# Two layers and a mixture of experts on one core: tables in steps, splits per residual chunk, both token tiles normalised in turn

## The chip, the core and the metric

The kernel runs on one core of a Trainium2 chip. Five engines work side by side, each through its own queue in order: TensorE (PE: matmuls and transposes into PSUM), VectorE (DVE), ScalarE (ACT), GpSimd (POOL), and SyncE (SP), which issues the transfers. The metric is the device time of one execution in microseconds (us), as the median of several runs; lower is better.

## The reference

256 tokens of width 1024 go through two layers and then a second block, all in float32.

```python
for l in range(DEPTH):                       # first block, DEPTH = 2
    x = x + 0.5 * swiglu_ffn(rms_norm(x, ffn1_norm[l]), ...)   # width 2816
    h = rms_norm(x, mix_norm[l]); proj = h @ w_in[l]
    y_ret = retention(...)                   # 4 heads of 128, rotary, decay
    y_mla = mla_attention(...)               # 8 heads, 64 + 32 rotary, causal
    x = x + jnp.concatenate([y_ret, y_mla], axis=-1) @ w_o[l]
    x = x + 0.5 * swiglu_ffn(rms_norm(x, ffn2_norm[l]), ...)
# second block
attn_o = bidir_gqa(...)                      # 8 query heads, 2 key heads of 64
hgrn_o = hgrn2_bidir(...)                    # gated recurrence, two directions
x = x + (sigmoid(gate_a) * (attn_o @ w_a) + sigmoid(gate_b) * (hgrn_o @ w_b)) @ w_out
x = x + hier_moe(rmsnorm(x, g_ffn), ...)     # 32 experts, top 2
```

## The kernel before

The residual x stays in SBUF as `XT`, features on the partitions (8 chunks of 128), tokens (two tiles of 128) along the free dimension. Weights come in as float32, 1 MB at a time, into four `raw` buffers (`loaded`, L314, issued on SP). `pieces` (L322) splits each into a high part on ACT (`wh`, L332) and a low part, the difference (`wl`, L342), on DVE; in the mixers POOL takes a share of the low part. Four buffers each of `wh` and `wl` lie between the splits and TensorE. Inputs are split the same way: `norm_parts` (L447) multiplies each chunk of `XT` by its gain, ACT writing the high part (L452) and DVE the low part (L453).

The order of the text goes `ffn`, `mixer1`, `ffn` for each layer, then `mixer2` and `moe`. The text alone doesn't fix the queues: a planner runs the instructions through a timeline of its own, and of those that are ready there it takes the one that stands first in the text. Each engine then works through the order so made, strictly in turn.

`ffn` (L493) goes through 11 slices of 256 columns (`f2`), a gate product and an up product in each; `to_residual` (L465) adds the down product to `XT` in four steps of two chunks (L487), squares of the new residual following on POOL (`square`, L408). In the first `ffn` a generator, `load_small` (L160), brings in constants, gains, broadcast rows and router weights, one step per slice from `HOOK_AT` (slice 3) on, each step's transfers placed on SP behind the last weight load issued. Its last step issues three transfers of router weights (L202 to L204) and calls `rotary` (L234), which loads the positions (L235), casts them (L238) and computes sine and cosine tables in some 60 small DVE instructions.

`mixer1` (L552) runs two generators against each other (`interleave`, L304): `mla`, the latent attention, is the main one, and after each of its steps `retention` goes on by about one piece of projection. In `mla` each token tile in turn is normalised (squares on POOL, L641 and L646; sums on DVE, L643 to L647; a reciprocal root by Newton's steps on DVE, `rms_rows`, L399 to L404), rotated (L651 to L660), and transposed on TensorE (`heads_T`, L607). Then come scores, maximum (L688, L689), scaling of the maximum (L690), exponentials, transposes of the probabilities, and their copies out of PSUM (`pt`: L718 on ACT, L719 on DVE). `retention` projects queries and keys, rotates them (`rot`, L740: L745 on POOL, L747 and L748 on DVE, tile `rx`) and transposes them at once.

`mixer2` (L824) does likewise with `attention` (L862), `recurrence` (L1201) and, as filling, `projections`. `mains` takes `NORM_AT` (3) steps of `attention`, then alternates `attention` and `recurrence`; `RATIO_2` (0.4) is the number of projection pieces per step. `recurrence` first pulls the projections that it needs itself. In `attention` each token tile is normalised, rotated, transposed, and copied to `qT` and `kE` (L897 to L904) before the next.

## Time and profile before

| | us |
|---|---|
| median of three runs (1723.22 to 1726.77) | 1724.34 |
| the profiled execution, its own time | 1726.29 |
| its span, first to last instruction | 1724.5 |
| TensorE busy | 1666.9 (97%) |
| DVE busy | 1028.5 (60%) |
| ACT busy | 700.4 (41%) |
| POOL busy | 481.4 (28%) |
| the layers, about | 0 to 1035 |
| mixers of the layers, about | 215 to 332 and 716 to 833 |
| mixer of the second block, about | 1035 to 1250 |
| experts, to the end | from 1250 |

The profile is that of one execution. Busy time is the share of a stretch in which an engine works; the view of waits sums what an engine waited for, by the instruction that released it; the timeline lists instructions in order, with the idle time before each and its releaser in brackets. A wait is put down to the releaser that came last. `PEclk` is the clock granted to TensorE, as a share of its full 2.4 GHz; 0.50 is the lower of its two levels, 1.2 GHz.

### The profile page before, as it was taken

Reading aid. Unit: us, or ns where it says so; the run is one execution under the profiler, and the core shown is the slowest. Engines: PE = TensorE matmul, PEld = TensorE weight load, DVE = VectorE, ACT = ScalarE, POOL = GpSimd, SP = SyncE. Lnnn points to the kernel's source line nnn. Section 1 sums busy time; section 2 is a strip of 40 time slices with the busy share of each in tenths; the row PEclk is TensorE's granted clock in tenths of the full one; section 3 lists DMA queues with packets and bytes.
Section 4 is the critical chain, followed back from the end, with each engine's and each line's share of the span. In section 5 each row is a group of like instructions: output and inputs, shape, how many; then the busy total and the mean of one; then the engine's idle time right before and its main releaser. Section 6 shows DMA issues by size and latency. Waiting matters only on the chain.

```text
span 1724.5 us, 23921 instructions
## 1 busy us (share of the span) xinstructions
PE 1666.9 (97%) x9393; PEld 1258.6 (73%) x9393; DVE 1028.5 (60%) x1631; ACT 700.4 (41%) x1079; POOL 481.4 (28%) x388
## 2 busy tenths in 40 slices
PE   8899988999999999989999999899999999999997
PEld 6788877788888888867888889889844444444442
DVE  6796788876667666787876669975632122122111
ACT  5554465465545554555555445654310000000001
POOL 6333365332222222553422144544400000000000
PEclk9999999999999999999999999999999999999999
DMA  9556542466566555543565555334999999999994
GB/s 313 167 176 198 162 159 83 151 195 190 169 203 182 184 189 173 163 130 100 173 194 190 183 185 166 109 99 147 398 379 400 422 421 422 421 421 422 421 422 178
DMA packets 216600, 407.80 MB, mean 236 GB/s; under 512 B 10063, under 2 KB 177190, under 8 KB 192166
## 3 DMA queue, kind: packets, MB, share of 16 engines
q1 hardware_dynamic: 216486, 406.25, 65.4%
q8 instruction: 75, 1.23, 0.3%
q14 instruction: 39, 0.32, 0.1%
HBM read 405.18 MB, written 1.05 MB: 236 GB/s over the span
## 4 chain that ended last, share of the span: by engine, by line
PE 79%; DVE 14%; issue 3%; POOL 2%; ACT 1%; SPq 1%; DMA 1%; DVEq 0%; POOLq 0%; ACTq 0%
PE mm L360 28%; PE mm L363 14%; PE aux L1507 14%; PE aux L1554 7%; DVE wl L342 4%; PE aux L1490 4%; PE mm L284 2%; PE mm L285 2%; PE mm L286 2%; PE mm L1579 2%; PE aux L123 1%; ACT wh L332 1%; POOL gu L509 0%; DVE XT L487 0%; DVE rx L747 0%
## 5 line engine op out<-in xcount | busy, mean ns | idle before, releaser
L342 DVE TENSOR_TENSOR wl<-raw,wh 128x1024 fp32r<-128x1024 f32 (+5 forms) x392 | 485.3, 1240 | 198.0 <-ACT wh L332 194.4
L332 ACT ACTIVATE wh<-raw 128x1024 fp32r<-128x1024 f32 (+3 forms) x392 | 405.1, 1036 | 356.8 <-PE mm L360 198.6
L360 PE MATMUL mm<-x,wh 128*128 128x512 f32 x1456 | 484.1, 398 | 11.5 <-DVE gu L380 6.5
L363 PE MATMUL mm<-x,wl 128*128 128x256 f32 x1456 | 361.4, 282 | 0.0
L360 PEld LDWEIGHTS mm<-x,wh 128*128 128x128 f32 x1456 | 271.1, 189 | 76.6 <-DVE gu L380 7.6
L363 PEld LDWEIGHTS mm<-x,wl 128*128 128x128 f32 x1456 | 256.0, 189 | 4.2
L360 PE MATMUL mm<-h,wh 128*128 128x512 f32 x704 | 246.6, 393 | 0.0
L1507 PE MATMUL aux<-raw,xg 128*64 128x512 f32 x1024 | 242.1, 598 | 0.0
L509 POOL TENSOR_TENSOR gu<-gu,rb 128x512 f32<-128x512 f32 x88 | 142.0, 1618 | 322.8 <-DVE gu L380 299.7
L363 PE MATMUL mm<-h,wl 128*128 128x256 f32 x704 | 196.4, 279 | 0.0
L1507 PEld LDWEIGHTS aux<-raw,xg 128*64 128x64 f32 x1024 | 76.2, 137 | 137.1 <-issue 131.9
L360 PEld LDWEIGHTS mm<-h,wh 128*128 128x128 f32 x704 | 131.9, 187 | 31.3
L342 POOL TENSOR_TENSOR wl<-raw,wh 128x352 fp32r<-128x352 f32 (+2 forms) x90 | 119.5, 1334 | 84.3 <-ACT wh L332 76.1
L363 PEld LDWEIGHTS mm<-h,wl 128*128 128x128 f32 x704 | 131.9, 187 | 0.0
L1554 PE MATMUL aux<-raw,hd 128*64 128x512 f32 x512 | 124.8, 594 | 0.0
L383 ACT ACTIVATE yp<-aux 128x512 fp32r<-128x512 f32 x32 | 19.1, 597 | 245.8 <-PE aux L1554 231.2
L1492 DVE TENSOR_TENSOR xg<-aux,gperm 128x256 f32<-128x256 f32 x64 | 27.0, 423 | 142.6 <-PE aux L1490 142.6
L1554 PEld LDWEIGHTS aux<-raw,hd 128*64 128x64 f32 x512 | 42.2, 137 | 69.1 <-issue 66.5
L1490 PEld LDWEIGHTS aux<-gg,hk 128*128 128x128 f32 x512 | 61.6, 196 | 31.0 <-issue 29.8
L285 PE MATMUL mm<-wl,x 128*128 128x512 f32 (+2 forms) x208 | 79.6, 386 | 2.6 <-DVE wl L342 2.5
L384 DVE TENSOR_TENSOR yp<-aux,yp 128x512 fp32r<-128x512 f32 x32 | 22.1, 691 | 97.2 <-ACT yp L383 97.2
L284 PE MATMUL mm<-x,wh 128*128 128x256 f32 x272 | 79.3, 292 | 0.0
(400 smaller groups left out, 2364.3 us busy)
## 6 DMA issues: line engine op xcount, KB each, us to landing
raw<-in_w_exp_gate_dram SPq DMA_DIRECT2D x64, 1024.0 KB
raw<-in_w_exp_up_dram SPq DMA_DIRECT2D x64, 1024.0 KB
raw<-in_w_exp_down_dram SPq DMA_DIRECT2D x62, 1024.0 KB
raw<-in_ffn_w_up_dram SPq DMA_DIRECT2D x44, 1024.0 KB
raw<-in_ffn_w_gate_dram SPq DMA_DIRECT2D x43, 1024.0 KB
raw<-in_w_in_dram SPq DMA_DIRECT2D x36, 1024.0 KB
raw<-in_ffn_w_down_dram SPq DMA_DIRECT2D x32, 1024.0 KB
raw<-in_ffn_w_down_dram SPq DMA_DIRECT2D x16, 768.0 KB
```

Of the source, the lines that this page charges most:

```text
L284: nc.tensor.matmul(ps, a[0], b[0], start=first, stop=False, skip_group_check=True)
L285: nc.tensor.matmul(ps, a[0], b[1], start=False, stop=False, skip_group_check=True)
L286: nc.tensor.matmul(ps, a[1], b[0], start=False, stop=last, skip_group_check=True)
L332: nc.scalar.activation(h, r[:, k0:k1], AF.Copy)
L342: eng.tensor_tensor(lf, rf, hf.bitcast(F32), op=ALU.subtract)
L360: nc.tensor.matmul(banks[j], lhs, chunk_both(xp, kk), start=kk == 0, stop=False, skip_group_check=True)
L363: nc.tensor.matmul(banks[j][:, :S], lhs, chunk(xp, kk)[0], start=False, stop=kk == k_all - 1, skip_group_check=True)
L509: nc.gpsimd.tensor_tensor(e, e, twice(rb), op=ALU.mult)
L1490: nc.tensor.matmul(ps[:, i], hk[:, t, (k0 + i) * P:(k0 + i + 1) * P], gs[t], start=i == 0 and t == 0, stop=i == 1 and t == 1, skip_group_c ...
L1507: nc.tensor.matmul(ps[half(s)], xg[:, k, half(s)], w[s][:, k % 4], start=k == 0, stop=k == 7, skip_group_check=True)
L1554: nc.tensor.matmul(pss[hf][half(s)], hd[:, ff, half(s)], w[s][:, ff - ks.start, hf * 512 - c0:(hf + 1) * 512 - c0], start=ff == 0, stop=ff ...
L1579: nc.tensor.matmul(osum[t][hf], gt[:, t * P:(t + 1) * P], yp[part][:, hf], start=False, stop=p == NP - 1 and part == 1, skip_group_check=True)
```

## The change

- `load_small` starts at slice 2 (`HOOK_AT`), yields between the router's transfers and the tables, and `rotary` is a generator itself: one step for the positions and first reductions, one for the second, one for each of cosine and sine, one for the copies.
- `norm_parts` is divided: `into_parts` splits one chunk. `to_residual` gets the next stage's gain and calls it for the two chunks that it has just finished, before their squares. `norm_parts` does what is left.
- In `mla` the norms of both tiles come first, then both rotations (with `kf`), then the transposes of both. The factor of the scores goes into the gain of the queries; the maximum comes out negated; `ptb` is copied by ACT.
- In `retention` the transposes of `rx` are put off (`turns`) and run after the first piece of the next projection.
- In `attention` of the second block both tiles are normalised, then both rotated, then both transposed. The factor goes into the copy to `qT`; the copies to `kx` and `kE` go from DVE to ACT; the maximum comes out negated. `NORM_AT` is 6, and the steps under it run at `RATIO_N` = 1.5 pieces each.
- In the recurrence a factor goes from two products into `homs`, so that two `scalar_tensor_tensor` in each direction become `tensor_tensor`.

```diff
+RATIO_N = 1.5
-HOOK_AT = 3
-NORM_AT = 3
+HOOK_AT = 2
+NORM_AT = 6
...
         late.update(cst=cst, gcol=gcol, rw=rw, gperm=gperm)
+        yield
 
         nc.gpsimd.tensor_tensor(rw, rw, gains("g_ffn_2", 0)[:, :, None].to_broadcast([P, 8, 40]), op=ALU.mult)
-        rotary()
+        yield from rotary()
...
             nc.vector.scalar_tensor_tensor(n1, nh, -4096.0, n1, op0=ALU.mult, op1=ALU.add)
+            yield
             for c in parts:
...
             for i, (shift, add) in enumerate(((0.25, math.pi / 2), (0.0, 0.0))):
+                yield
                 whole(n1, ang, 1 / (2 * math.pi), shift)
...
+    parts_of, ahead = {}, []
+
+    def into_parts(g, k):
+
+        if k == 0:
+            parts_of["x"] = [pair_tile(np_, [P, 4, S], "x%d" % i, bufs=1) for i in range(2)]
+        xh, xl = chunk(parts_of["x"], k)
+        x = x_banks[k // 2][:, k % 2] if x_banks else XT[:, k]
+        nc.scalar.activation(xh, x, AF.Copy, scale=g[:, k:k + 1])
+        nc.vector.scalar_tensor_tensor(xl, x, g[:, k:k + 1], xh.bitcast(F32), op0=ALU.mult, op1=ALU.subtract)
+
...
+            if g is not None:
+                for k in (2 * d2, 2 * d2 + 1):
+                    into_parts(g, k)
+                    ahead.append(k)
             if final:
                 square(2 * d2)
...
                     rms_rows(ms, 32.0, 24)
-                    yield
+                    mss.append(ms)
+                    yield
+                for t in range(2):
+                    q, kv, ms = qs[t], vv[t], mss[t]
...
-                    yield
                     nc.vector.tensor_tensor(kf[t][:, :, 0:64], kv[:, :, 0:64], ms[:, 8:16, None].to_broadcast([P, 8, 64]),
                                             op=ALU.mult)
-                    heads_T(qT, q, t, "qn_nope")
+                    yield
+                for t in range(2):
+                    heads_T(qT, qs[t], t, "qn_nope")
                     yield
                     heads_T(kT, kf[t], t, "kn_nope")
                     yield
...
-                    nc.vector.tensor_reduce(mx[:, 0:2], s0, axis=AX.X, op=ALU.max)
-                    nc.vector.tensor_reduce(mx[:, 2:4], s1, axis=AX.X, op=ALU.max)
-                    nc.vector.tensor_scalar(mx[:, 0:4], mx[:, 0:4], -scale, None, op0=ALU.mult)
+                    nc.vector.tensor_reduce(mx[:, 0:2], s0, axis=AX.X, op=ALU.max, negate=True)
+                    nc.vector.tensor_reduce(mx[:, 2:4], s1, axis=AX.X, op=ALU.max, negate=True)
...
-                    nc.vector.tensor_copy(ptb, tb)
+                    nc.scalar.activation(ptb, tb, AF.Copy)
...
-                    ps2 = aux_bank().rearrange("p (h t) -> p h t", h=4)
-                    for h in range(4):
-                        flip(ps2[:, h], x[:, h], ident)
-                    nc.scalar.activation(dst[:, :, t * P:(t + 1) * P], ps2, AF.Copy)
+
+                    def turn():
+                        ps2 = aux_bank().rearrange("p (h t) -> p h t", h=4)
+                        for h in range(4):
+                            flip(ps2[:, h], x[:, h], ident)
+                        nc.scalar.activation(dst[:, :, t * P:(t + 1) * P], ps2, AF.Copy)
+                    turns.append(turn)
...
+            def then_turns(gen):
+
+                for i, _ in enumerate(gen):
+                    while i == 0 and turns:
+                        turns.pop(0)()
+                    yield
...
-                    nc.vector.tensor_copy(kx, x[:, 8:10][:, ::-1])
+                    nc.scalar.activation(kx, x[:, 8:10][:, ::-1], AF.Copy)
...
-                    nc.vector.tensor_copy(kE[0:64, :, 0, ts], ps[0:64, 0:2])
-                    nc.vector.tensor_copy(kE[64:128, :, 1, ts], ps[64:128, 0:2][:, ::-1])
-                    yield
+                    nc.scalar.activation(kE[0:64, :, 0, ts], ps[0:64, 0:2], AF.Copy)
+                    nc.scalar.activation(kE[64:128, :, 1, ts], ps[64:128, 0:2][:, ::-1], AF.Copy)
+                    yield
...
-                nc.vector.scalar_tensor_tensor(flat(qp), flat(hq), scale, flat(qp), op0=ALU.mult, op1=ALU.mult)
+                nc.vector.tensor_tensor(qp, hq, qp, op=ALU.mult)
...
                 rec = recurrence()
+                rate[0] = RATIO_N
                 for _ in range(NORM_AT):
                     next(att)
                     yield
+                rate[0] = RATIO_2
```

## Rows read from the trace of the kernel before

**Rows 1.** The page's totals: busy us, share of the span, instructions, by engine.

```profile
PE 1666.9 (97%) x9393; PEld 1258.6 (73%) x9393; DVE 1028.5 (60%) x1631; ACT 700.4 (41%) x1079; POOL 481.4 (28%) x388
```

**Rows 2.** Stretches: start:end, length, busy per engine, granted clock, DMA share, GB/s.

```profile
80.00:82.00 2.00, 1.52 (x4) 1.23 (x5) 1.97 (x5) 0.00 (x0) 1.17 (x1) 0.50 0.70 170
...
240.00:260.00 20.00, 17.09 (x74) 13.28 (x75) 19.83 (x38) 8.22 (x9) 13.43 (x11) 0.99 0.41 132
258.00:262.00 4.00, 2.53 (x10) 2.32 (x11) 3.96 (x5) 1.25 (x2) 3.99 (x4) 0.69 0.00 0
272.00:284.00 12.00, 12.00 (x83) 10.57 (x82) 5.05 (x11) 5.22 (x8) 2.97 (x3) 1.00 0.16 49
400.00:420.00 20.00, 20.00 (x115) 17.41 (x114) 13.42 (x17) 11.54 (x18) 5.17 (x4) 1.00 0.64 203
768.00:772.00 4.00, 4.00 (x22) 3.76 (x21) 3.72 (x14) 2.75 (x5) 0.44 (x1) 0.57 0.43 133
1092.00:1096.00 4.00, 4.00 (x20) 3.91 (x19) 3.93 (x6) 3.97 (x6) 3.09 (x2) 0.53 0.58 170
...
1128.00:1132.00 4.00, 4.00 (x22) 3.19 (x21) 2.58 (x4) 2.28 (x6) 2.36 (x2) 0.50 0.06 9
1400.00:1420.00 20.00, 20.00 (x98) 9.32 (x99) 3.87 (x10) 1.10 (x3) 0.00 (x0) 1.00 1.02 424
```

**Rows 3.** Timeline, 64 to 84 us: start, us, engine, line, [idle before, releaser]; SP, DVE, PE.

```profile
64.57 5.16 SPq L202 DMA_DIRECT2D gperm<-in_g_ffn_dram  x1
...
73.72 2.13 SPq L235 DMA_DIRECT2D posi<-in_positions_dram  x1
...
77.59 0.19 DVE L238 CAST pos<-posi 128x2 f32<-128x2 int32 x1 [6.65 <-DMA posi<-in_positions_dram]
...
80.48 3.78 PE L360 MATMUL mm<-x,wh 128*128 128x512 f32 x8 [4.88 <-DVE gu L380]
```

**Rows 4.** TensorE's waits, 205 to 345 us: total, times, longest.

```profile
PE aux L123 <- DVE q L660: 2.9, 2, 2.7
...
PE aux L123 <- DVE rx L748: 1.4, 2, 0.7
PE mm L728 <- DVE pt L719: 1.3, 1, 1.3
```

**Rows 5.** The same for 700 to 845 us.

```profile
PE aux L123 <- DVE rx L748: 5.1, 3, 3.4
...
PE mm L728 <- DVE pt L719: 1.1, 1, 1.1
```

**Rows 6.** The same for 1020 to 1245 us.

```profile
PE aux L913 <- DVE kE L903: 5.0, 1, 5.0
PE aux L123 <- DVE mx L917: 3.3, 1, 3.3
...
PE aux L123 <- DVE kx L899: 1.3, 1, 1.3
```

**Rows 7.** DVE by line and shape, whole span: count, busy us, mean ns, idle before.

```profile
L719 DVE COPY pt<-aux 128x256 f32<-128x256 f32 x8 | 3.3, 413 | 0.0
...
L690 DVE TENSOR_SCALAR mx<-mx 128x4 f32<-128x4 f32 x8 | 2.5, 313 | 0.1
...
L903 DVE COPY kE<-aux 64x256 f32<-64x256 f32 x2 | 0.8, 408 | 0.0
```

**Rows 8.** Timeline, 255 to 263 us, POOL and DVE.

```profile
255.66 3.38 POOL L745 TENSOR_TENSOR rt<-rx,sinr 128x512 f32<-128x512 f32 x2
...
257.85 1.23 DVE L404 SCALAR_TENSOR_TENSOR nwy<-nwt,nwy 128x24 f32<-128x24 f32 x1
...
262.45 0.17 DVE L404 SCALAR_TENSOR_TENSOR nwy<-nwt,nwy 128x24 f32<-128x24 f32 x1
```

**Rows 9.** Timeline, 326 to 335 us, DVE and PE.

```profile
326.28 1.37 DVE L453 SCALAR_TENSOR_TENSOR x<-XT,gcol,x 128x256 fp32r<-128x256 f32 x2
...
334.21 0.50 PE L360 MATMUL mm<-x,wh 128*128 128x512 f32 x1 [1.07 <-DVE x L453]
```

More of the change, by code (lines that the diff above doesn't have):

```diff
@@ L445, in row_broadcast @@
         return rb
-    def norm_parts(g):
-        xp = [pair_tile(np_, [P, 4, S], "x%d" % i, bufs=1) for i in range(2)]
-        for k in range(8):
-            xh, xl = chunk(xp, k)
-            x = x_banks[k // 2][:, k % 2] if x_banks else XT[:, k]
-            nc.scalar.activation(xh, x, AF.Copy, scale=g[:, k:k + 1])
-            nc.vector.scalar_tensor_tensor(xl, x, g[:, k:k + 1], xh.bitcast(F32), op0=ALU.mult, op1=ALU.subtract)
+    parts_of, ahead = {}, []
[6 more added lines that the diff above has]
+        nc.vector.scalar_tensor_tensor(xl, x, g[:, k:k + 1], xh.bitcast(F32), op0=ALU.mult, op1=ALU.subtract)
+    def norm_parts(g):
+        for k in range(len(ahead), 8):
+            into_parts(g, k)
+        ahead.clear()
         for k2, b in enumerate(x_banks):
@@ L463, in wview, with to_residual @@
         return w.rearrange("(k p) n -> p k n", p=P)
-    def to_residual(wsrc, kc, yp, scale, final=True, between=None):
+    def to_residual(wsrc, kc, yp, scale, final=True, between=None, g=None):
         src = wview(wsrc)
@@ L521, in ffn @@
                         next(hook, None)
-            run(to_residual(wd, 22, hp, 0.5))
+            run(to_residual(wd, 22, hp, 0.5, g=g_next()))
     def proj_tok(wsrc, c0, n, xp, use):
@@ L566, in mixer1 @@
                 gtab[nm] = (tcos, tsin)
+            gcols = {"qn_nope": m.tile([P, 1], F32, name="gqs", bufs=1), "kn_nope": gains("kn_nope", l, 1)}
+            nc.gpsimd.tensor_scalar(gcols["qn_nope"], gains("qn_nope", l, 1), 96.0 ** -0.5, None, op0=ALU.mult)
             cmask = m.tile([P, P], BF16, name="cmask", bufs=1)
@@ L612, in heads_T @@
                     nc.scalar.activation(dst[:96, h0:h0 + 4, t * P:(t + 1) * P], ps[:96], AF.Copy,
-                                         scale=gains(gname, l, 1)[:96])
+                                         scale=gcols[gname][:96])
             def mla():
@@ L667, in mla @@
                     yield
-                scale = 96.0 ** -0.5
                 po = None
@@ L766, in retention @@
                 yield
-                yield from proj_tok(w_in, 512, 512, xp, rot(rkT))
+                yield from then_turns(proj_tok(w_in, 512, 512, xp, rot(rkT)))
                 yield
-                yield from proj_tok(w_in, 1024, 512, xp, use_v)
+                yield from then_turns(proj_tok(w_in, 1024, 512, xp, use_v))
                 yield
@@ L820, in mixer1 @@
             share[0] = 0.0
-            run(to_residual(w_o[512:], 4, yp[1:], 1.0))
+            run(to_residual(w_o[512:], 4, yp[1:], 1.0, g=gains("ffn2_norm", 8 * l)))
     def mixer2():
@@ L874, in attention, with room @@
                 nc.gpsimd.memset(kE, 0.0)
+                mss = []
+                def room():
+                    return m.tile([P, 16, 64], F32, tag="A1", name="xr", bufs=1)[:, :10]
                 for t in range(2):
-                    ts = slice(t * P, (t + 1) * P)
-                    x = xa[t]
-                    xr = m.tile([P, 16, 64], F32, tag="A1", name="xr", bufs=1)[:, :10]
+                    x, xr = xa[t], room()
                     nc.gpsimd.tensor_tensor(xr, x[:, 0:10], x[:, 0:10], op=ALU.mult)
@@ L882, in attention @@
                     rms_rows(ms[:, :10], 64.0, 10)
-                    nc.vector.tensor_tensor(x[:, 0:10], x[:, 0:10], ms[:, :10, None].to_broadcast([P, 10, 64]),
+                    mss.append(ms)
+                    yield
+                for t in range(2):
+                    x, xr = xa[t], room()
+                    nc.vector.tensor_tensor(x[:, 0:10], x[:, 0:10], mss[t][:, :10, None].to_broadcast([P, 10, 64]),
                                             op=ALU.mult)
-                    yield
                     for nm, hs, n in (("q_norm_2", slice(0, 8), 8), ("k_norm_2", slice(8, 10), 2)):
@@ L893, in attention @@
                     yield
+                for t in range(2):
+                    x, ts = xa[t], slice(t * P, (t + 1) * P)
                     ps = aux_bank().rearrange("p (a t) -> p a t", a=4)
@@ L970, in mixer2 @@
             nc.vector.tensor_tensor(hup, hom, lb, op=ALU.add)
+            homs = m.tile([P, 2, 4], F32, name="homs", bufs=1)
+            nc.vector.tensor_scalar(homs, hom, scale, None, op0=ALU.mult)
             def times_sigmoid(z, i):
@@ L1086, in direction @@
                 nc.scalar.activation(qi, b, AF.Exp)
[L1087 removed]
+                nc.vector.tensor_tensor(qi, hq, qi, op=ALU.mult)
                 dd = m.tile([P, 4, 4], F32, name="dd")
```

27 lines of the change are left out of this document (14 added, 13 removed).

## Prediction

> **What bounds the kernel now.** I read four views in this order. The totals of the page come first: TensorE is busy for 1666.9 of 1724.5 us, DVE for 60% of the span [rows 1]. A span that is 97% matmul can't be shortened by saving work on other engines in general; it can lose only the 57.6 us in which TensorE has nothing to do, and the time in which it works at its lower clock. So the second view is the table by stretches [rows 2]: the last part of the span (row 1400:1420) has TensorE busy without a gap and the DMA share at 1.02. That part, the experts, is fed by weight transfers without pause, and the change doesn't touch it. Its first loads wait for the memory of the stage ahead of it, so what is saved ahead of it should reach the end of the span one for one. The feed-forward stretches have no idle TensorE at all (row 400:420, with 20.00 of 20; the 18 rows of that view from 340 to 700 us are alike in this). What remains is the start, the two mixers of the layers and the mixer of the second block. There the row 240:260 shows DVE at 19.83 of 20 us while TensorE is idle for 2.9: DVE sets the pace in those stretches, not in the mean of 60%. The third view is the list of waits of TensorE in the three mixers [rows 4 to 6]; the fourth is the timeline around the longest of them.
>
> **The start: tables in steps.** DVE runs its queue in order. The first instruction of the rotary tables, the cast L238, waited 6.65 us for the transfer of the positions, which stood at the end of a row of small transfers on SP: the first was issued at 64.57 and took 5.16 us to issue, the positions were issued from 73.72 to 75.85 [rows 3]. Splits of weights stood behind that cast, and TensorE stood still for 4.88 us; after that it ran at a granted clock of 0.50, the lower of its two levels (row 80:82 of [rows 2]), where the next 3.78 us did the work of 1.9. So the event costs 4.9 + 1.9 = 6.8 us. The change puts a step between these transfers and the positions, so that the slow issues go behind the weights of one slice and the positions behind those of the next. HOOK_AT goes from 3 to 2, so the transfers ahead of it (constants, gains, rows) each come one slice earlier. With the 11.3 us of issue (64.57 to 75.85) shortened to the 2.13 us of the positions alone, the cast should find its data or wait about 1 us. The tables' instructions stay the same in number and are spread over five slices; what stands behind them on DVE is the next split, which now meets one fifth of them at a time. Each SP transfer that is moved forward goes behind a weight load, and four raw buffers keep the loads up to two slices ahead of their use, so I cost the move at 0; if that cover is gone, I bound it by the 4.9 us that the old order lost. POOL's multiplication of the router's weights moves a step behind its transfers and so waits for less. I take 6 of the 6.8 us.
>
> **Input splits per residual chunk.** This moves 8 ACT and 8 DVE instructions per normalisation from the text behind the residual to the text within it, five times. The rows say that the planner had already done so: the L453 of the next stage ran at 326.28, 5 us ahead of the end of the residual, and only one wait of 1.07 us is left behind it [rows 9]. I cost this at 0, with bounds of -1 and +1 us at each of the two places where a mixer ends (elsewhere there is no wait to gain). The squares run on POOL and keep their place there; the sum that waits for them is needed two products later.
>
> **The mixers of the layers.** Two things change: the transposes of the rotated queries and keys (rx) go a step behind, after the first piece of the next projection, and both token tiles are normalised before either is transposed. The waits that answer to it are 2.9 (q L660), 1.4 (rx) and 1.3 (pt) in the first layer [rows 4], 5.1 (rx) and 1.1 (pt) in the second [rows 5]. The granted clock adds to this. In 258:262 it was 0.69: a share of (1 - 0.69)/0.5 = 0.62 of 4 us at half speed, half of which is lost, 1.2 us; in 768:772 it was 0.57, by the same way 1.7 us [rows 2]. That makes 5.6 + 1.2 = 6.8 and 6.2 + 1.7 = 7.9 us. The pt waits should go: the copy L719 leaves DVE for ACT (8 x 0.413 us), and the scaling L690 is gone (8 x 0.313) [rows 7]. The other waits are only half real. DVE was full in that stretch, so moving a transpose back lets TensorE go on only as long as split weights lie ready; beyond that it waits for splits instead. What speaks for a gain is the slack behind the stretch: in 272:284 DVE was busy for 5.05 of 12 us [rows 2], and in the new order 32 transposes that need no DVE fall there. I take half: 3.4 and 4.0 us, with bounds from -6 (below) to the full 14.7.
>
> Here one rule speaks against the change. A reciprocal-root step of 0.17 us took 1.23 us while POOL's rt L745 ran from 255.66 to 259.04 [rows 8]. The Trainium skill (SBUF — State Buffer, Who interferes with whom) says that an instruction of DVE with two inputs in SBUF waits out a POOL instruction that reads SBUF, whole, and the other way round. The trace agrees for that one. By that rule, taking both tiles' squares on POOL next to each other, with two chains of small steps on DVE, would lengthen these chains rather than hide them; by it alone the mixers would give nothing or lose. That is the second rival.
>
> **The mixer of the second block.** TensorE waited 5.0 us for kE L903, 3.3 at mx L917 and 1.3 for kx [rows 6]; the clock of 0.53 in 1092:1096 and of 0.50 in 1128:1132 [rows 2] adds 1.9 and 2.0. Together 13.5 us. The change takes kE and kx off DVE (ACT writes them; two copies L903 of 0.41 us [rows 7], and two L904 of the same shape) and drops the eight scalings L917 (half of L690's shape, so under 0.3 us each). It normalises both tiles in the first six steps, against 1.5 pieces of projection each (before: three steps at 0.4, the rest among the recurrence). The number of pieces ahead of the recurrence is the same, since it pulls the projections that it needs itself; but the second tile's norm leaves the crowded stretch. The four scale-and-multiply instructions become plain products of the same size: 0. I expect the kE wait to go nearly whole (5.0 + 1.9, take 5), kx 1, and of the later stall, which is a full DVE and not one copy, 1. Sum 7 us, bounds 0 and 13.5. ACT, which takes over the copies, was itself full in 1092:1096 (3.97 of 4) [rows 2]; hence 5 of the 6.9.
>
> **The sum.** 6 + 0 + 3.4 + 4.0 + 7 = 20.4 us. The profiled execution took 1726.29 us, 1.8 more than its span; that gives 1705.9. The median of the three runs lies 2.0 below that execution, so the forecast is **1704 us**.
>
> **The rivals.**
> First, *the waits move*: DVE stays the bound in all mixers, and TensorE waits for splits where it waited for transposes. Then only the start (6) and about half of the work that DVE loses count: 3.3 (L719) + 2.5 (L690) + 1.6 (L903, L904) = 7.4, half 3.7. Time 1724.3 - 9.7, about 1715. For it: DVE at 19.83 of 20. Against it: the slack right behind.
> Second, *slower*: the two chains of norms in turn keep DVE from splitting. A chain has 13 small steps; at 1.23 instead of 0.17 us each it is 13.8 us longer, which is the bound; at half of that 6.9, with the lower clock's 1.7, 8.6 us per layer. Two layers: 17.2, against the 13 us of start and second block: 1724.3 - 13 + 17.2 = 1728.5. It decides from 6.5 us per layer on. Against it: the chain of the second tile already ran beside the first's in the trace, since the L404 at 257.85 [rows 8] is one of its steps and stands between the first tile's rope instructions.
> Third, *the change does not do what it says*: each queue's order is made by a planner from its own timeline, and the text only sets priorities. If the cast keeps its place behind an earlier gap and the mixers their order, only the 3.7 us of DVE work are saved: 1721.
> Fourth, *all of it*: every wait named goes, with its clock: 6.8 + 6.8 + 7.9 + 13.5 = 35.0, time 1689.
>
> **How the numbers follow.** Forecast (1697 to 1711) 0.47; waits move (1711 to 1718) 0.20; all of it (1687 to 1697) 0.14; doesn't do it (1717 to 1722) 0.09; slower (1726 to 1740) 0.10. The range 1690 to 1722 leaves out the slower case and some of the best one. A change of 0.2% (3.4 us) is about what a measurement of this kernel can tell from none. Faster by more than that: 0.85 (the forecast, the waits moved and all of it make 0.81, and about half of the case at 1721); within it 0.06; slower 0.09.
>
> **What would show it.** Right: no wait of DVE for the positions beyond 2 us and no granted clock under 1 near 80 us; rx, q and kE gone from TensorE's waits; the experts' stage as long as before and begun about 20 us earlier. Wrong: waits of TensorE for wl L342 in the mixers in place of the others; small steps of DVE (L402 to L404) with a longer mean; the lower clock at new places; loads of the first feed-forward that land late because constants went ahead of them.

## The result, and the profile after

The changed kernel took **1737.14 us** (median of six, 1732.01 to 1737.74), the kernel before in the same session 1724.3 (six, 1723.22 to 1726.77). The ratio is 1.0068, with a 95% interval from 1.0058 to 1.0079: **slower** by 0.7%, where 1704 was forecast and 1722 was the upper end. The profiled execution took 1736.47 us, its span is 1734.7. Below, each ratio is against the kernel before as run on the same chip beside the experiment; its profile is always the one of 1724.5 us.

DVE and POOL did get less work, as [rows 1] against the totals after show: DVE 1028.5 to 1019.8 us, POOL 481.4 to 476.6. ACT, which took over copies, went from 700.4 to 705.5.

```profile
PE 1672.2 (96%) x9393; PEld 1264.9 (73%) x9393; DVE 1019.8 (59%) x1602; ACT 705.5 (41%) x1093; POOL 476.6 (27%) x390
```

TensorE's 9393 instructions are as many as before, but it was busy 5.3 us longer, and the clock below shows why. To see where, I took the end of each stage's last product and read one row per stage (these ends are exact; the table of times had put the mixers at about 215 and 1035). The columns are those of [rows 2]. The rows are, in order: first feed-forward from 20 us on, mixer of layer 0, mixer of layer 1, mixer of the second block up to the router. The kernel before:

```profile
20.00:206.66 186.66, 180.07 (x1018) 156.81 (x1017) 137.90 (x206) 92.11 (x140) 65.86 (x45) 0.98 0.62 195
206.66:331.85 125.19, 115.45 (x616) 93.90 (x614) 105.09 (x182) 69.71 (x131) 66.69 (x60) 0.99 0.40 129
707.17:831.62 124.45, 115.45 (x616) 94.61 (x614) 102.94 (x182) 69.89 (x131) 69.61 (x60) 0.99 0.41 130
1020.07:1251.85 231.78, 219.14 (x1636) 205.56 (x1634) 181.35 (x298) 112.49 (x161) 113.05 (x90) 0.97 0.53 186
```

The changed kernel:

```profile
20.00:209.34 189.34, 180.49 (x1018) 156.69 (x1017) 138.02 (x206) 92.31 (x139) 65.45 (x45) 0.98 0.61 193
209.34:337.18 127.84, 116.92 (x615) 96.46 (x614) 102.39 (x174) 71.00 (x135) 67.80 (x61) 0.96 0.39 126
712.37:837.32 124.95, 116.11 (x615) 95.56 (x614) 100.64 (x174) 71.51 (x135) 69.36 (x61) 0.97 0.41 129
1025.65:1262.99 237.34, 222.39 (x1635) 207.91 (x1634) 177.79 (x285) 114.42 (x167) 107.95 (x90) 0.96 0.54 191
```

The differences of the lengths are +2.7 (start), +2.7, +0.5 and +5.6 us; the other feed-forwards together and the experts gave back 0.2 and 1.0. That is the 10.2 us by which the spans differ. Length less busy is idle time: it grew by 2.3, 1.2 and 2.3 us in the first, second and fourth stage and was the same in the third (9.0 and 8.8). The rest, 0.4, 1.5, 0.7 and 3.3 us, is busy time. Summed over rows of 2 us as busy time times (1 - granted clock), what the lower level took went from 1.4 to 4.7 us in the first mixer, from 1.5 to 3.1 in the second and from 5.6 to 8.8 in the third. That is an estimate, and in the layers' mixers more than the busy time grew by; it shows that the clock is enough to explain it. Each kernel has one profile here, and two profiles of the same queues differ by up to 1.5 us in such a stage (last section), so the stages only point at the places; the experiments decide.

**The start.** The cast still waits. Timeline of the changed kernel (SP, DVE, PE), to be held against [rows 3]:

```profile
53.96 4.70 SPq L203 DMA_DIRECT2D gperm<-in_g_ffn_dram  x1
...
62.38 2.00 SPq L324 DMA_DIRECT2D raw<-in_ffn_w_gate_dram  x1
64.48 0.53 SPq L324 DMA_DIRECT2D raw<-in_ffn_w_up_dram  x1
65.06 1.42 SPq L237 DMA_DIRECT2D posi<-in_positions_dram  x1
...
73.93 0.17 DVE L240 CAST pos<-posi 128x2 f32<-128x2 int32 x1 [4.55 <-DMA posi<-in_positions_dram]
...
75.08 2.08 PE L365 MATMUL mm<-x,wh 128*128 128x512 f32 x4 [4.99 <-DVE gu L385]
...
119.41 2.22 PE L365 MATMUL mm<-x,wh 128*128 128x512 f32 x8 [1.08 <-DVE gu L385]
```

The stretch in which the positions were under way, and TensorE's waits from 40 to 130 us (total, times, longest):

```profile
66.00:74.00 8.00, 4.09 (x26) 3.51 (x24) 1.90 (x3) 2.12 (x4) 1.51 (x2) 0.91 1.09 350
...
PE mm L365 <- DVE gu L385: 7.3, 5, 5.0
```

The positions were issued 8.7 us earlier than before, and behind two weight loads of 1 MB each, issued at 62.38 and 64.48. Their issue ended at 66.48; the cast ran 7.4 us later, at 73.9. Before, their issue ended at 75.85, the last weight load ahead of them had been issued at 64.14, and the cast ran at 77.59. Issued 8.7 us earlier, they let the cast run only 3.7 us earlier. DVE came to it 1.6 us earlier and waited 4.55 us instead of 6.65, and TensorE stood still as long as before, 4.99 us against 4.88. The Trainium skill (DMA: Bandwidth & Descriptors, Queues, rings and completion order) says that each of the 16 engines takes the descriptors of SP's transfers in ring order. By that rule a small transfer has its turn behind the megabytes ahead of it. The trace agrees in the main: in 66 to 74 us the transfers moved 350 GB/s, at which 2 MB take 6.0 of the 7.4 us (an estimate).

That explains why nothing was gained. The loss is in what follows: where one wait of 4.9 us was all before, four more of 0.21 to 1.08 us come behind it, up to the one at 119.41, 7.3 us in all. They make the 2.3 us of idle time by which this stage grew.

**The mixers.** TensorE's waits in the changed kernel (total, times, longest), from 205 to 345 us, against [rows 4]:

```profile
PE aux L124 <- DVE rx L770: 6.0, 3, 4.6
PE aux L124 <- DVE y L841: 3.1, 2, 1.9
```

and from 1020 to 1270 us, against [rows 6]:

```profile
PE aux L124 <- DVE pb L964: 10.4, 3, 4.8
...
PE aux L955 <- ACT kE L946: 0.2, 1, 0.2
```

Of the waits that the prediction named, those for q (2.9), kE (5.0, now 0.2), kx and mx are gone. The one for pt is gone in the first layer (1.3); in the second it went from 1.1 to 0.9 us, now for ACT's copy. The wait for rx, named too, is not gone: it grew from 1.4 to 6.0 us in the first layer and stayed at 5.1 in the second. New are waits for y, the output of the retention, in the layers, and for pb, the probabilities, in the second block.

### The profile page after: what moved, and what is told of

The parts are those of the page before. It is cut to its first block, busy times and chain, and to the rows that moved or that the text cites. A ratio compares the mean times of both kernels' runs of the same rounds, so it can differ in the third digit from the quotient of the medians.

```text
span 1734.7 us, 23889 instructions
## 1 busy us (share of the span) xinstructions
PE 1672.2 (96%) x9393; PEld 1264.9 (73%) x9393; DVE 1019.8 (59%) x1602; ACT 705.5 (41%) x1093; POOL 476.6 (27%) x390
## 4 chain that ended last, share of the span: by engine, by line
PE 82%; DVE 11%; issue 2%; POOL 2%; ACT 2%; DMA 1%; SPq 0%; DVEq 0%; POOLq 0%; ACTq 0%
PE mm L365 28%; PE mm L368 14%; PE aux L1553 14%; PE aux L1600 7%; PE aux L1536 4%; DVE wl L347 4%; PE mm L291 3%; PE mm L289 3%; PE mm L290 3%; PE mm L1625 2%; PE aux L124 2%; ACT wh L337 1%; POOL gu L526 1%; DMA posi<-in_positions_dram 1%; PE aux L708 0%
## 5 line engine op out<-in xcount | busy, mean ns | idle before, releaser
L347 DVE TENSOR_TENSOR wl<-raw,wh 128x1024 fp32r<-128x1024 f32 (+5 forms) x392 | 490.8, 1254 | 209.3 <-ACT wh L337 204.8
L291 PE MATMUL mm<-wh,x 128*128 128x512 f32 (+2 forms) x208 | 79.7, 385 | 0.0
L289 PE MATMUL mm<-wh,x 128*128 128x512 f32 (+2 forms) x208 | 79.2, 392 | 0.3 <-ACT wh L337 0.3
```

The costliest lines, as they stand in the source:

```text
L289: nc.tensor.matmul(ps, a[0], b[0], start=first, stop=False, skip_group_check=True)
L291: nc.tensor.matmul(ps, a[1], b[0], start=False, stop=last, skip_group_check=True)
L347: eng.tensor_tensor(lf, rf, hf.bitcast(F32), op=ALU.subtract)
```

## The experiments

All are the kernel before with one part of the change, unless they say otherwise.

**Three parts, each alone.** First the start:

```diff
-HOOK_AT = 3
+HOOK_AT = 2
...
+        yield
 
         nc.gpsimd.tensor_tensor(rw, rw, gains("g_ffn_2", 0)[:, :, None].to_broadcast([P, 8, 40]), op=ALU.mult)
-        rotary()
+        yield from rotary()
```

> The kernel before with only the start of the change: load_small in more steps, the rotary tables as a generator, HOOK_AT 2. Theory: the start's loss is of this part alone. The positions now go behind the weights of one more slice and wait for their transfers (after: issued 65.06 to 66.48, landed at 73.93, a wait of 4.55 us on DVE), and the tables' steps then meet a DVE without slack until 116 us. So the first feed-forward ends about 2.7 us later (209.3 instead of 206.7), nothing changes later, time +2.7 us, about 1727. Rival: the loss at the start comes from the splits per residual chunk, and the steps by themselves gain what was forecast: first feed-forward ends at about 201, time about 1718.

Measured: 1727.81 us, ratio 1.0018 (1.0008 to 1.0028); the first feed-forward ended at 208.47, and TensorE's waits up to 130 us were 6.3 us in four pieces. The loss at the start belongs to this part.

Then all edits to the layers' mixers:

```diff
+                for t in range(2):
+                    q, kv, ms = qs[t], vv[t], mss[t]
...
-                    nc.vector.tensor_scalar(mx[:, 0:4], mx[:, 0:4], -scale, None, op0=ALU.mult)
...
-                    nc.vector.tensor_copy(ptb, tb)
+                    nc.scalar.activation(ptb, tb, AF.Copy)
...
+                    turns.append(turn)
```

> The kernel before with all edits to the mixer of the layers (both tiles normalised, then rotated, then transposed; transposes of rx a step behind; ptb copied by ACT; the scaling of the maximum folded away), and nothing else. Theory: this part alone makes what the two mixers lost in the changed kernel: first mixer 127.8 us from the end of its feed-forward instead of 125.2, second 125.0 instead of 124.5; time +3 us, about 1727. Rival: the mixer's loss in the changed kernel came from another part (input splits per chunk, or the later start); then these edits give 0 to -7 us, time 1717 to 1724.

Measured: 1728.27 us, ratio 1.0019 (1.0009 to 1.0029). Waits in the first mixer as in the changed kernel: rx 6.0, y 3.1; its length was 127.57 us, that of the second 124.24. But the profiled execution was the fastest of the ten, 1722.89 us, so the profile doesn't show what the median lost.

And all edits to the second block's mixer:

```diff
+RATIO_N = 1.5
...
-NORM_AT = 3
+NORM_AT = 6
...
+                    mss.append(ms)
+                    yield
...
+                    nc.scalar.activation(kE[0:64, :, 0, ts], ps[0:64, 0:2], AF.Copy)
```

> The kernel before with all edits to the mixer of the second block (both tiles normalised in the first six steps, at 1.5 pieces each; kE and kx copied by ACT; factors folded), and nothing else. Theory: this part makes the 5.3 us that the stage lost: from 231.5 to about 237 us between the end of the last feed-forward and the router, since the softmax of the attention now runs at the same time as the recurrence's large instructions (TensorE waited 10.4 us for pb); time +5, about 1729. Rival: the loss came from the input splits per residual chunk or from what stood before; then the stage takes 224 to 231 us and the time is 1717 to 1724.

Measured: 1731.24 us, ratio 1.0042 (1.0025 to 1.0059), with waits for pb of 10.5 us in a stage of 234.89. The excesses of the three parts add up to 0.79%, the whole change has 0.68%: within the intervals the loss is theirs.

**The residual chunks.**

```diff
+            if g is not None:
+                for k in (2 * d2, 2 * d2 + 1):
+                    into_parts(g, k)
+                    ahead.append(k)
```

> The kernel before; the only edit is the input splits per finished residual chunk. Theory: nothing changes, since the planner had put these splits there already: ratio 0.9993 to 1.0007, the same wait of 1.1 us for x behind each layer's mixer. Rival: it costs 1 to 2 us where the other parts' sum (1.0018, 1.0019 and 1.0042) is over the whole (1.0068), that is, the parts don't add: ratio under 0.999.

Measured: 1.0000 (0.999 to 1.0009). That term of the sum, 0, holds, and for the reason given: in the trace every engine has the same instructions in the same order as in the kernel before.

**The start: positions or steps.** The transfer alone is moved:

```diff
             cst.append((lo, hi, t))
+        nc.sync.dma_start(posi, A["positions"].rearrange("o (t p) -> p (o t)", p=P))
         yield
...
     def rotary():
-        nc.sync.dma_start(posi, A["positions"].rearrange("o (t p) -> p (o t)", p=P))
```

> The kernel before; the only edit is that the transfer of the positions is issued in the first step of load_small, with the constants, instead of in the last. Theory: the cast of the positions then finds its data, TensorE's wait of 4.88 us and the stretch at half clock behind it (1.9 us) go, the first feed-forward ends near 200 instead of 206.7 and the time is 5 to 7 us less, about 1718. Rival: DVE has no slack between 84 and 120 us, so the tables' 60 instructions are late next: TensorE idles there in pieces, and the first feed-forward ends at 204 to 207, time 1722 to 1724.

Measured: 1722.03 us, ratio 0.998 (0.9969 to 0.9992); the first feed-forward ended at 203.48. Its timeline (DVE, PE):

```profile
64.50 0.16 DVE L238 CAST pos<-posi 128x2 f32<-128x2 int32 x1
...
83.94 1.19 PE L360 MATMUL mm<-x,wh 128*128 128x512 f32 x4 [1.45 <-DVE gu L380]
```

The cast waits for nothing and no lower clock shows in this stage. But TensorE now waits in four pieces (0.75, 1.45, 0.47 and 0.50, together 3.2 us between 71 and 114) where it waited once for 4.9. The theory was right about the wait and the clock, the rival about the pieces and the time: the event is worth 3.2 us in the end of the stage. That the rest of its 6.8 is the tables' own work fits the rows, in which DVE is busy for 28.9 of the 30 us from 80 to 110, but no run isolates it.

Then the same with the steps of the change (the two diffs above together, except that the positions' line goes):

> The start of the change (more steps, HOOK_AT 2) and the positions issued with the constants. Theory: the steps lost only because the positions' transfer stood behind two megabytes of weights; with the positions early the cast finds its data and the start is no worse than with the positions early and the old steps (0.998): ratio 0.996 to 0.998, first feed-forward ends at 201 to 203.5. The tables' instructions stand one or two between two splits with the old steps already, so the steps by themselves change nothing there. Rival: the steps by themselves lose (transfers moved ahead of weights, waits of 2.3 us in pieces from 94 to 120 us): ratio 0.999 to 1.001, first feed-forward ends at 204 to 206.

Measured: 0.9981 (0.9971 to 0.9991), end of the first feed-forward 204.20: the same ratio as without the steps. The ratio is just above the theory's range, the end lies in the rival's. The steps by themselves show no worth. The traces show why: from the cast on, two to six instructions of the tables stand between two splits with the steps, and two to six did before.

**The layers' mixers, edit by edit.** The turns:

```diff
-                yield from proj_tok(w_in, 512, 512, xp, rot(rkT))
+                yield from then_turns(proj_tok(w_in, 512, 512, xp, rot(rkT)))
```

> The kernel before; the only edit is that the transposes of rx in the retention of the layers go a step behind (turns). The layer mixers' edits together gave 1.0019. Theory: this edit loses: a transpose that stands behind the next piece of projection still waits for an rx that DVE finishes late (6.0 us of waits for rx in the first mixer with all edits, 1.4 before), and the piece in between takes splits from the same DVE. Waits for rx 4 to 6 us per mixer in place of rx and q, ratio 1.001 to 1.002 (2 to 3 us slower). Rival: the loss is of the order of the norms in mla, and the turns by themselves take away 1 to 3 us of waits: ratio 0.998 to 0.9995.

Measured: 1.0000 (0.9991 to 1.001). Neither theory nor rival: rx keeps 1.4 us in the first mixer and has 4.6 in the second (5.1 before), q grows from 2.9 to 4.4, and the stages stay as long (125.20 and 124.75).

The order of the norms:

```diff
-                    yield
+                    mss.append(ms)
+                    yield
+                for t in range(2):
+                    q, kv, ms = qs[t], vv[t], mss[t]
```

> The kernel before; the only edit is the order in mla of the layers: both tiles normalised, then both rotated, then transposed. Theory: the loss is of the turns, so this edit by itself is within 0.1% of the kernel before; the q wait of 2.7 us becomes smaller and another wait takes its place. Rival: the two chains of norms in turn hold up DVE's splits and rotations; TensorE idles 11 us and more in the first mixer instead of 9.3 to 9.9, ratio 1.001 to 1.002.

Measured: 1729.23 us, ratio 1.0027 (1.0016 to 1.0037); the first mixer took 129.58 us, with 10.4 idle. The six microseconds of rx come from this edit (waits, then three stretches of that kernel):

```profile
PE aux L123 <- DVE rx L753: 6.0, 3, 4.7
PE aux L123 <- DVE y L812: 1.2, 1, 1.2
```

```profile
296.00:300.00 4.00, 2.67 (x18) 1.51 (x16) 2.79 (x8) 4.00 (x13) 1.71 (x3) 1.00 0.81 253
300.00:304.00 4.00, 2.79 (x17) 2.36 (x18) 3.26 (x5) 1.65 (x3) 0.69 (x1) 0.75 0.41 139
304.00:308.00 4.00, 4.00 (x16) 3.11 (x14) 1.76 (x4) 0.60 (x2) 0.00 (x0) 0.50 0.00 0
```

The prediction's own picture of this loss, longer small steps, isn't what is seen: those on 128x24 (L399 to L404 of the kernel before) took 16.1 us in all here, 16.7 before and 17.0 in the changed kernel. One wait of 4.7 us for rx replaces those for q and for the step behind it, and a second spell of low clock follows 40 us later. Of the 4.4 us by which the stage is longer, idle time has 0.7; the rest is busy time, at the lower clock. Why the order costs that second spell was not isolated.

Copies and folded factors of all three mixers, without a change of order or pace (the layers' two are shown below):

```diff
-                    nc.vector.tensor_copy(kx, x[:, 8:10][:, ::-1])
+                    nc.scalar.activation(kx, x[:, 8:10][:, ::-1], AF.Copy)
```

> The kernel before with only the copies that move from DVE to ACT (ptb, kx, kE) and the factors folded away (scaling of the maxima, gain of the queries, qT, homs) in all three mixers; no order or pace is changed. Theory: less work on DVE shortens the mixers a little, since DVE is full there: 7.4 us of DVE work less, of which about a third shows: ratio 0.997 to 0.999 (2 to 5 us), waits for pt and kE gone. Rival: the planner reorders around it and the gain is lost in new waits: ratio 0.9995 to 1.002.

Measured: 1728.74 us, ratio 1.0023 (1.0013 to 1.0032): the rival, a little above its range. The second block's mixer became shorter, 227.8 us, and the layers' mixers longer, 131.3 and 127.4. So the layers' part was divided once more. The copy:

```diff
-                    nc.vector.tensor_copy(ptb, tb)
+                    nc.scalar.activation(ptb, tb, AF.Copy)
```

> The kernel before; the only edit is that the second half of the transposed probabilities (ptb, L719) is copied out of PSUM by ACT instead of DVE. Theory: this copy is what made the layers' mixers slower in the run with copies and folds (there 131.3 and 127.4 us for the two mixers, 125 to 127.5 and 124.5 before): ACT also writes the high parts of the weights, the exponentials and the gate of the retention, and the gate comes late, so TensorE waits for y (3.5 us) with a stretch of low clock behind it. Ratio 1.002 to 1.004, waits for y of 2 to 4 us in the first mixer. Rival: the folded factors are to blame, by reordering the queues; then this edit takes away the pt waits (1.3 and 1.1) and gives 0.998 to 1.000.

Measured: 1722.44 us, ratio **0.9983** (0.9974 to 0.9993). The theory fell, the copy gains: the mixers took 123.53 and 122.58 us, and TensorE's waits for DVE's copy [rows 4, rows 5] are gone; 0.7 us per layer for ACT's are left. The folds:

```diff
-                                         scale=gains(gname, l, 1)[:96])
+                                         scale=gcols[gname][:96])
...
-                    nc.vector.tensor_reduce(mx[:, 0:2], s0, axis=AX.X, op=ALU.max)
+                    nc.vector.tensor_reduce(mx[:, 0:2], s0, axis=AX.X, op=ALU.max, negate=True)
...
-                    nc.vector.tensor_scalar(mx[:, 0:4], mx[:, 0:4], -scale, None, op0=ALU.mult)
```

> The kernel before; the only edit is that the factor of the scores in the layers goes into the gain of the queries and the maximum comes out negated (eight scalings of 0.31 us less on DVE, nothing moved to ACT). Theory: ratio 0.998 to 1.0005, since it takes work away and moves none; the stages as before. Rival: the order of the queues shifts with it and the y waits of 3.5 us come from here: ratio 1.001 to 1.003.

Measured: 1733.16 us, ratio **1.0044** (1.0028 to 1.0059). Eight instructions of 0.31 us are taken away and the kernel gets 7.6 us slower by the ratio; the mixers took 130.30 and 128.89 us. The timelines show how. The kernel before (PE: last product of the gate's projection, then the third pair of scores; ACT: the gate):

```profile
292.89 0.39 PE L286 MATMUL mm<-wh,x 128*128 128x512 f32 x1
...
293.67 0.39 PE L679 MATMUL aux<-kT,qT 96*128 96x128 f32 x2
...
291.92 0.69 ACT L760 ACTIVATE rg<-mm,rs 128x512 f32<-128x512 f32 x1 [0.39 <-PE mm L286]
```

With the folds alone (PE, ACT; L681 is the score, L694 the exponentials):

```profile
290.99 0.39 PE L681 MATMUL aux<-kT,qT 96*128 96x128 f32 x2
...
295.08 0.40 PE L286 MATMUL mm<-wh,x 128*128 128x512 f32 x1
...
300.74 1.09 PE L123 MATMUL aux<-ident,y 128*128 128x128 f32 x4 [3.65 <-DVE y L807]
...
295.62 0.37 ACT L694 ACTIVATE pb<-aux,mx 128x128 f32<-128x128 f32 x1 [3.72 <-DVE mx L690]
...
297.21 0.70 ACT L760 ACTIVATE rg<-mm,rs 128x512 f32<-128x512 f32 x1
```

and its stretches behind that wait:

```profile
300.00:304.00 4.00, 2.57 (x12) 1.51 (x12) 3.90 (x5) 2.29 (x5) 1.22 (x1) 0.50 0.15 38
304.00:308.00 4.00, 3.95 (x15) 3.25 (x16) 1.71 (x3) 1.40 (x5) 0.00 (x0) 0.50 0.27 95
```

The scores went ahead of the gate's last products. Their exponentials waited 3.72 us on ACT for the maximum, and the gate stood behind them, 5.3 us later than before, and y with it. TensorE waited 3.65 us for y, and worked at half clock behind the wait. To separate this order from the folding itself, the scaling was put back as a multiplication by -1. In the trace of that kernel all queues stand in the order of before; only POOL has one more small instruction per layer, which makes the new gain:

```diff
+                    nc.vector.tensor_scalar(mx[:, 0:4], mx[:, 0:4], -1.0, None, op0=ALU.mult)
```

> The folds of the layers as in the run with folds alone (factor of the scores in the gain of the queries), but the eight scalings of the maximum stay on DVE, with the factor -1; every engine's queue then has the order of the kernel before. Theory: the folds lose by the order alone: without the scaling the planner has the maxima ready earlier and puts the third pair of scores ahead of the last 12 products of the gate's projection, so that y is late. With the order of before the ratio is 0.9993 to 1.0007, and the wait of 3.65 us for y is gone. Rival: the folding itself costs (the gain computed on POOL, the exponentials without a factor): ratio 1.003 to 1.005.

Measured: 1.0010 (1.0001 to 1.002). The waits for y are gone, and so is 0.34 of the 0.44%: the order is the cause of most of it. A tenth of a per cent may remain with the folding; its interval begins at 0.01%, and I leave that open.

**The second mixer's pace.** All its edits, with the old pace:

```diff
-RATIO_N = 1.5
+RATIO_N = 0.4
...
-NORM_AT = 6
+NORM_AT = 3
```

> The second block's mixer with all its edits, but with the pace of before: NORM_AT 3 and 0.4 pieces per step there, instead of 6 and 1.5. Theory: the loss (1.0042 with all edits) is of the pace: with all six steps ahead, the softmax of the attention falls together with the recurrence's large instructions on DVE and POOL. With the old pace the waits for pb are under 3 us (10.4 with all edits), TensorE idles 12 to 13 us in the stage instead of 15, and the ratio is 0.998 to 1.001. Rival: the order itself (both tiles normalised before one is transposed) loses, and the ratio stays at 1.003 to 1.005.

Measured: 0.9998 (0.9988 to 1.0007), waits for pb 3.1 us and idle time 12.0. The pace made the loss. The changed kernel's timeline at the place (DVE, POOL, ACT, PE) shows by what:

```profile
1089.47 2.86 DVE L964 TENSOR_TENSOR pb<-pb,mx 128x512 f32<-128x512 f32 x1
1092.25 1.93 DVE L347 TENSOR_TENSOR wl<-raw,wh 128x672 fp32r<-128x672 f32 x1
...
1095.98 3.43 DVE L1045 TENSOR_SCALAR sg<-sn,hom,hup 128x256 f32<-128x256 f32 x2
1099.33 0.68 DVE L958 TENSOR_REDUCE mx<-aux 128x2 f32<-128x512 f32 x1
...
1103.07 0.69 DVE L964 TENSOR_TENSOR pb<-pb,mx 128x512 f32<-128x512 f32 x1
...
1089.41 2.37 POOL L1088 TENSOR_TENSOR kp<-kp,sn 128x1024 f32<-128x1024 f32 x1 [1.55 <-ACT kp L1086]
...
1094.94 3.37 POOL L1103 TENSOR_TENSOR ks<-ks,sn 128x1024 f32<-128x1024 f32 x1
...
1100.52 1.28 ACT L961 ACT_TABLE_LOAD   x1
...
1103.90 1.09 PE L124 MATMUL aux<-ident,pb 128*128 128x128 f32 x4 [4.83 <-DVE pb L964]
```

With six steps ahead, the softmax runs beside the recurrence's large products. The product pb took 2.86 us beside L1088 on POOL and 0.69 with POOL free, and a split of 128x672 behind it took 1.93 us (0.84 at 1099.93, with POOL free). Two L1045 took 3.43 us beside L1103. The maximum for the second pair of probabilities (L958) stood behind all of it on DVE, at 1099.33; their exponentials then waited for ACT, which first loaded a table for 1.28 us. The rule that the prediction quoted (the Trainium skill, SBUF — State Buffer, Who interferes with whom) is borne out for the product and the split, two-input instructions of DVE beside POOL; at the norms, where the prediction expected it, the small steps grew by 0.3 us in all.

The order of the norms in this mixer has a price too. This kernel and the one at the end that keeps only what gained have the same second mixer but for that order. The stage, with the order and without it:

```profile
1019.77:1250.48 230.71, 218.71 (x1635) 205.23 (x1634) 177.78 (x285) 113.96 (x167) 113.72 (x90) 0.98 0.53 187
...
1012.70:1240.47 227.77, 216.79 (x1636) 203.62 (x1634) 177.34 (x285) 115.34 (x167) 110.59 (x90) 0.99 0.54 189
```

The two kernels below that keep it have 230.7 and 230.8 us, the one with copies and folds, without it, 227.8. So here too the new order seems to have taken back what the copies and folds gained, some 2.9 us; why wasn't isolated.

**Do the causes account for the whole?** The changed kernel less the folds of the layers, the norm order and the new pace, that is with these lines as before:

```diff
-RATIO_N = 1.5
+RATIO_N = 0.4
...
-NORM_AT = 6
+NORM_AT = 3
...
-                    mss.append(ms)
...
+                    nc.vector.tensor_scalar(mx[:, 0:4], mx[:, 0:4], -scale, None, op0=ALU.mult)
```

> The whole change less three of its edits: the folds of the layers, the norm order in mla, and the pace of the second mixer (NORM_AT 3 and 0.4 pieces as before). The start, the splits per residual chunk, the turns, ptb on ACT and the second mixer's copies, folds and order stay. Theory: the parts measured alone add: 1.0018 (start) - 0.0017 (ptb) - 0.0002 (second mixer at the old pace) + 0 (turns, residual splits): ratio 0.999 to 1.001, against 1.0068 of the whole change. Rival: the parts react on each other through the planner, and the ratio stays at 1.003 or more.

Measured: 1723.41 us, ratio 0.9993 (0.9983 to 1.0003), against 1.0068 of the whole. And with the positions early as well (the diff of the positions above):

> As the run of the change less three, and the positions' transfer is issued with the constants. Theory: the start then turns from 1.0018 to 0.9981, as alone: ratio 0.9955 to 0.9975, 0.37% under the change less three. Rival: in the full change the start's loss is of the slower transfers ahead of the weights, and the ratio is 0.998 to 1.000.

Measured: 1718.57 us, ratio 0.9964 (0.995 to 0.9978). Both came as expected.

**Only what gained:** positions early, ptb on ACT, and in the second mixer the copies and folds without its order and pace, each by its diff above.

> The kernel before with only what gained: the positions' transfer with the constants (0.998), ptb copied by ACT (0.9983), and in the second mixer the copies on ACT and the folded factors without a change of order or pace (its stage took 227.8 us in the run with copies and folds, 230 to 232 elsewhere). Theory: they add: 0.994 to 0.996, about 1716 us, faster than both kernels. Rival: the second mixer's stage of 227.8 us was chance of one execution, and the ratio is 0.996 to 0.9975.

Measured: **1715.16 us**, ratio 0.9947 (0.9931 to 0.9964), faster than both kernels and in the theory's range. The totals:

```profile
PE 1659.3 (97%) x9393; PEld 1254.3 (73%) x9393; DVE 1021.3 (60%) x1610; ACT 705.4 (41%) x1093; POOL 479.8 (28%) x388
```

The first feed-forward ends at 203.71, the mixers take 122.65, 122.67 and 227.77 us.

## Why the prediction was wrong, step by step

- **What bounds the kernel**: right. The span moved with TensorE's idle time and clock in the start and the three mixers, and the experts' end followed almost one for one (472.7 us from the router to the end before, 471.7 after). The sum rests on that, so its error is in the terms.
- **Start, -6**: wrong in sign (+0.18%, 3.1 us). The step that failed is "with the 11.3 us of issue shortened to the 2.13 us of the positions alone, the cast should find its data or wait about 1 us". It counted the time of issue and left out the bytes ahead: with 2 MB in front the wait was 4.55 us. A second step failed with it: that the tables' instructions would be "spread over five slices". Two to six of them stood between two splits before and after, so the steps spread nothing. The term was too large besides: with no wait at all the stage gains 3.2 us, not 6.8. (Its part for the clock was read from eight products; summed over rows of 2 us it is 2.5 us, not 1.9.) Why TensorE's four further waits of 2.3 us came with the steps, where the kernel before had none, stays open.
- **Residual chunks, 0**: right, 1.0000.
- **Layers' mixers, -3.4 and -4.0**: wrong in sign (+0.19%). The waits for q and, in the first layer, pt did go; the step "I take half" failed, since it priced only the waits that go and not those that a new order of the queues brings. Of its edits, ptb gained 0.17%, 2.9 us, about the two waits for pt (2.4), the turns nothing, the norm order lost 0.27% and the folds 0.44%. The folds had been priced as a saving of 8 x 0.313 us. Together these are 0.54%, not the 0.19% of all edits at once. In the first mixer the norm order and the folds each have their second spell of low clock from about 300 us on, and one stretch can lose it only once; that this is the reason is a reading, not a test. The lower bound of -6 us doesn't come out of the second rival, whose own sum for two layers is 17.2.
- **Second mixer, -7**: wrong in sign (+0.42%). The part on kE, kx and mx was right, and copies and folds alone did shorten the stage, to 227.8 us from the 230 to 232 of kernels that leave it as it was. The failed step is "the second tile's norm leaves the crowded stretch": what came into the crowded stretch in its place, the softmax, was not asked for. It cost waits for pb of 10.4 us; with the old pace they are 3.1 and the loss is gone.
- **Rivals**: "slower" was given 10%, with one mechanism, norm steps lengthened beside POOL. The time fell into its range (1726 to 1740), but by luck: its mechanism is not the one measured. "The waits move" was right in that they move, and wrong in where to: it named the splits, and TensorE waited for rx, y and pb. It also left out that the new waits can be longer than the old ones.
- **Signs named beforehand**: of the signs of being right, the waits for q and kE went; DVE's wait for the positions (4.55 us, where 2 was the limit) and TensorE's for rx stayed. Of the signs of being wrong, waits of TensorE for wl in place of the others didn't show (1.1 us in the first mixer, 0.8 before); longer small steps hardly (17.0 us against 16.7); the lower clock at new places did (0.58 in 304 to 308 us).

## What to carry to other kernels

Where a planner makes the queues, an edit has two prices: its work, and the new order that the planner makes without it. Eight small instructions less cost 0.44% here, so compare the queues before pricing the instruction. A small transfer that is needed early belongs ahead of the large ones; a short issue is not enough. And taking work out of a crowded stretch only helps if what moves up in its place has room: look at what comes next in that queue.

## What the runs showed of the hardware that was not expected

The same work has longer and shorter spells of low clock. In the first mixer the run with only the second mixer's edits has the same order of work as the kernel before and nearly the same waits (q 2.7 and 2.7 us, the next 1.9 and 1.5), yet that stage took 127.55 us against 125.19. The stretches of the kernel before:

```profile
260.00:264.00 4.00, 2.67 (x10) 1.81 (x8) 3.96 (x7) 1.36 (x2) 1.99 (x3) 0.63 0.00 0
264.00:268.00 4.00, 3.86 (x22) 3.22 (x23) 3.97 (x10) 1.86 (x3) 0.55 (x1) 1.00 0.45 131
```

and of the other:

```profile
260.00:264.00 4.00, 2.09 (x9) 1.30 (x7) 4.00 (x8) 0.68 (x1) 1.09 (x2) 0.50 0.07 18
264.00:268.00 4.00, 4.00 (x12) 3.03 (x11) 3.97 (x8) 0.76 (x2) 1.05 (x1) 0.50 0.32 113
268.00:272.00 4.00, 4.00 (x22) 3.52 (x21) 2.61 (x4) 3.11 (x5) 1.02 (x1) 0.83 0.40 131
```

So 2.4 us of one stage of one profiled execution can be nearly all clock (the idle time differs by 0.2), almost as much as the +2.7 that the first mixer shows above.

The kernel with the residual chunks alone gives a cleaner measure, since its queues are those of the kernel before. Its first mixer and its second block's mixer:

```profile
206.51:332.80 126.29, 115.41 (x615) 94.16 (x614) 105.41 (x182) 69.67 (x131) 66.66 (x60) 0.99 0.40 128
1020.99:1251.27 230.28, 216.84 (x1635) 203.26 (x1634) 181.33 (x298) 112.55 (x161) 112.99 (x90) 0.99 0.53 187
```

The kernel before had 125.19 and 231.78 us, with 9.7 us idle in the first where this one has 10.9. With the same work in the same order, a stage's length differs by 1.1 to 1.5 us between two executions, and its idle time by 1.1. What an edit did is safer in the ratio of many runs than in one profile's stage.
